# First two products of the cross-attention queries taken by pairs of feature blocks, with other durations in the planner

## The chip, the cores and the metric

The kernel runs on one core of a Trainium2 chip. The metric is the device time of one execution in microseconds (us); for each kernel several executions are timed and the median is given. The engines are named as in the profile: PE is TensorE (PEld its weight loads), DVE is VectorE, ACT is ScalarE, POOL is GpSimd, and SP is SyncE, which issues the DMAs here. A row of the trace such as `L193 MATMUL` names the line of the kernel that issued the instruction.

## The reference

One layer of a streaming-encoder trunk, with batch 1, 1024 rows, width 1024, in float32: token mixing by two groups of attention heads, cross-attention into 256 memory tokens, and an MLP of width 4096. Each of the three is normalised before, normalised after and added to the residual. The change lies in the second part, and in what stands beside it:

```python
def memory_cross_attention(h, mem_n, w_mq, w_mk, w_mv, w_mo):
    q = (h @ w_mq).reshape(B, S, MEM_HEADS, MEM_HEAD_DIM)       # 1024 x 1024 by 1024 x 1024, 4 heads of 256
    k = (mem_n @ w_mk).reshape(B, M, MEM_HEADS, MEM_HEAD_DIM)   # M = 256 memory tokens
    v = (mem_n @ w_mv).reshape(B, M, MEM_HEADS, MEM_HEAD_DIM)
    logits = einsum('bshd,bmhd->bhsm', q, k) * MEM_HEAD_DIM ** -0.5
    p = softmax(logits, axis=-1)
    o = einsum('bhsm,bmhd->bshd', p, v).reshape(B, S, D_MODEL)
    return o @ w_mo

x = x + rmsnorm(y @ w_out, g_mix_post)                          # end of the token mixing
h = rmsnorm(x, g_mem_pre)
y = memory_cross_attention(h, mem_n, w_mq, w_mk, w_mv, w_mo)
x = x + rmsnorm(y, g_mem_post)
```

## The kernel before

**Numbers in two parts.** Every operand of a product is split into a high part and a low part of a reduced format (fp32r). ScalarE copies the high part out, VectorE subtracts it for the low part, and `mm3` (lines 191 to 195) does three matmuls for each piece of a product: high by high, high by low, low by high. Names with `hi`, `_h` or `qh` are high parts, those with `lo`, `_l` or `ql` low ones.

**Rows.** The 1024 rows are 8 tiles of 128, in two halves of four (`th` is 0 and 1). When the output projection of the token mixing is done for a tile, `close_row` finishes it: GpSimd takes the inverse root `rw{n}0` of its mean square, VectorE adds to the residual (`xtw{n}`), the result is stored, ScalarE sums its squares, GpSimd takes a second root `rw{n}1`, and ScalarE scales the row to `yw{n}` (for the second half `yw10` to `yw13`, for the tiles 4 to 7). A root is two kinds of instruction, on lines 1088 to 1091, on 128 numbers. `raw_steps` transposes these rows on PE (`tr_h2T`: four transposes to a PSUM tile), and ScalarE copies them out as the raw query operands `h2r`. A residual row is loaded by the pump `Rows` into one of two buffers `xt`.

**Query projection.** The product `h @ w_mq` is taken as a Strassen-type scheme over a 2 x 2 division of both sides: seven half-size products instead of eight, in the order

```python
QUERIES = (("A11", "B11"), ("A12", "B21"), ("A22", "T4"), ("S2", "T2"), ("S1", "T1"), ("S4", "B22"), ("S3", "T3"))
for p, (an, bn) in enumerate(QUERIES):
    for i in range(2):          # a weight block: two feature blocks
        for a in range(2):      # feature block nb = 2 * i + a, 512 query columns
            for kc in range(4): # yields, then one mm3
```

The A and S names are forms of the queries (A11, A12 of the first 512 rows, A22 of the second, S1 to S4 sums of them, made and split by the pump `Forms`), the B and T names forms of the weights. So `mq00` to `mq03` are the four feature blocks of A11 by B11, each of 12 wide matmuls (128 x 512); blocks 0 and 1 read the weight block `B11_0`, blocks 2 and 3 `B11_1`. `query_leave` empties the PSUM tile: for product 0 ScalarE copies it to `qm`, for product 1 VectorE adds the two (`qv`), and `query_final` makes `qh` and `ql` of that, the queries of the first half of rows for head 0 (blocks 0 and 1) and head 1 (blocks 2 and 3).

**Attention to the memory.** For each half, head h and row tile b, `memory_score_steps` does six matmuls (`ms{th}{h}{b}`, 128 x 256) into one of two PSUM banks; VectorE takes the maximum, ScalarE the exponential with its sum (`mp`; its end frees the bank), VectorE the reciprocal, and GpSimd multiplies `mp` by it. `memory_turn_steps` transposes the pairs of tiles on PE (`mtr{th}{h}{0,1}`) and splits them into `ph2` and `pl2`. `memory_out_steps` multiplies them by the values (`mo{h}{nb}`), `operand_parts` copies the result out (`ro`, `A11o`, S forms), and `strassen_steps` does the output projection by seven products again (`ym`).

**What sets the order.** The order of instructions on each engine is written out by a planner in Python (`Flow`, lines 56 to 119), which simulates the program while it emits it. PE's work is a list of streams in order of priority; the planner takes the first stream whose next step is ready by its own clock. Work for other engines is put with a duration and a level, and a waiting item goes to its engine when that is free, the lowest level first. Pumps issue loads and splits when buffers are free: `stock.pump` loads the weight blocks in the order of `Stock.blocks` (`wraw`), ScalarE and VectorE split them (`whi`, `wlo`), and the homes of the split tiles (`w`, `w`, `wq`) are dealt in turn by place in that list. `Tokens` counts free buffers. So a duration in the text of the program decides order alone; on the chip each engine takes its instructions as written, and waits by semaphore where an operand is late.

From the end of the output projection on the streams are, in order of priority: `memory_out_steps`, `memory_turn_steps`, `memory_score_steps`, `rstd_steps`, the second half's rows and its filler (with `query_steps`, `strassen_steps` among it).

## Time and profile before

| | before |
|---|---|
| median of 3 runs | 1456.9 us (1456.2 to 1458.52) |
| the profiled execution | 1457.35 us |
| its span | 1455.6 us |
| granted clock of PE | 0.999 |
| instructions | 21887 |
| matmuls and transposes recorded on PE | 7505 |
| DMA | 262.12 MB, mean 180 GB/s |

The span is the profiled execution from its first instruction to its last; the execution's own time stands 1.75 us above it. The page gives each engine's busy time as a share of the span. Sections of 40 equal slices show it over time; one slice is 36 us here, so the change, which lies between 600 and 790 us, covers five of them. Two views carry more than the page for so small a stretch: the busy time of each engine between given times (columns: stretch; its length; then for PE, PEld, DVE, ACT, POOL the busy time and the number of instructions; the granted clock; the share of the DMA engines; GB/s), and the instructions of one engine in order of time (start, duration of one, engine, line, output <- inputs, shape, how many in a row, and in brackets the idle time of the engine ahead of it with what ended it).

### The profile page before, as it was taken

What the parts mean: (1) busy time and instruction counts of PE and PEld (TensorE: products, weight loads), DVE (VectorE), ACT (ScalarE), POOL (GpSimd) and SP (SyncE); (2) the same over time, 40 slices, a digit from 0 to 9 for tenths busy, and PEclk for the clock granted to TensorE, in tenths of its full rate; (3) what the DMA queues carried; (4) which work ended last, traced back from release to release, by engine and by line L of the source; (5) the groups of instructions that cost most, each with busy time, mean ns of one, the idle gap of its engine ahead of it and who ended that gap; (6) DMA issues with size and microseconds to landing.
All of it is one profiled execution on the core that took longest, in us unless ns stands there. A gap on an engine that the chain in (4) does not pass through costs nothing. (4 is left out here: it accounts for less than half of the span.)

```text
span 1455.6 us, 21887 instructions
## 1 busy us (share of the span) xinstructions
PE 1436.3 (99%) x7505; PEld 1222.9 (84%) x7505; DVE 1123.1 (77%) x1894; ACT 871.2 (60%) x1509; POOL 390.4 (27%) x496
## 2 busy tenths in 40 slices
PE   9999999999999999989999999999999999999998
PEld 8988888888889888877878887888888888888886
DVE  6788787867677857778888787896666866789897
ACT  6567676766677835975566555555555555555553
POOL 1245465545554311430103511003223000000003
PEclk9999999999999999999999999999999999999999
DMA  7143433542425584452134646875545997786786
GB/s 276 49 128 83 127 81 127 158 124 55 115 59 152 172 307 171 178 184 73 59 102 159 220 143 227 284 241 188 174 166 193 307 343 249 250 280 234 276 287 205
DMA packets 109439, 262.12 MB, mean 180 GB/s; under 512 B 12280, under 2 KB 30720, under 8 KB 109328
## 3 DMA queue, kind: packets, MB, share of 16 engines
q1 hardware_dynamic: 109184, 260.47, 53.8%
q8 instruction: 59, 0.97, 0.3%
q14 instruction: 52, 0.43, 0.1%
q10 hardware_dynamic: 144, 0.26, 0.1%
HBM read 186.70 MB, written 65.59 MB: 173 GB/s over the span
## 5 line engine op out<-in xcount | busy, mean ns | idle before, releaser
L727 DVE TENSOR_TENSOR phl<-ptr,phl 128x512 fp32r<-128x512 f32 (+1 forms) x152 | 92.3, 615 | 30.9 <-ACT phl L730 29.7
L730 ACT ACTIVATE phl<-ptr 128x512 fp32r<-128x512 f32 (+1 forms) x152 | 79.6, 539 | 49.4 <-PE ptr L721 47.7
L2454 ACT ACTIVATE whif<-ra 128x1024 fp32r<-128x1024 f32 x45 | 47.6, 1058 | 77.3 <-PE fx L194 34.8
L2589 POOL TENSOR_SCALAR rf<-sf 128x1 f32<-128x1 f32 x7 | 7.0, 1002 | 313.3 <-ACT jf L2570 313.1
L764 PE MATMUL pv<-phl,vs 128*128 128x512 f32 (+1 forms) x304 | 86.0, 367 | 0.4 <-DVE phl L727 0.4
L2456 DVE TENSOR_TENSOR wlof<-ra,whif 128x1024 fp32r<-128x1024 f32 x45 | 55.0, 1222 | 35.9 <-ACT whif L2454 35.8
L193 PE MATMUL fx<-vhif,whif 128*128 128x512 f32 x168 | 65.6, 391 | 0.0
L194 PE MATMUL fx<-vlof,whif 128*128 128x512 f32 x168 | 65.6, 391 | 0.0
L195 PE MATMUL fx<-vhif,wlof 128*128 128x512 f32 x168 | 65.4, 389 | 0.0
L764 PEld LDWEIGHTS pv<-phl,vs 128*128 128x128 f32 x304 | 54.8, 188 | 10.5 <-DVE phl L727 1.4
L778 POOL TENSOR_TENSOR o<-o 64x256 f32<-64x256 f32 x64 | 47.9, 749 | 51.6 <-DVE o L776 34.9
L2305 POOL TENSOR_TENSOR sc<-wf,wf 128x512 f32<-128x512 f32 x8 | 12.8, 1599 | 177.0 <-DMA gi1S<-s 90.9
L1528 POOL TENSOR_SCALAR mp<-mp,mst 128x256 f32<-128x256 f32 x32 | 20.0, 634 | 128.3 <-DVE mst L1527 82.3
L193 PE MATMUL k<-hT_hi,whik 128*128 128x512 f32 x128 | 53.3, 416 | 0.0
L193 PE MATMUL q<-hT_hi,whiq 128*128 128x512 f32 x128 | 51.8, 405 | 0.0
L776 DVE TENSOR_TENSOR o<-pv,o 64x512 f32<-64x512 f32 x64 | 43.9, 686 | 9.9 <-ACT o L781 8.9
L193 PE MATMUL yw<-whiwo,yT_hi 128*128 128x512 f32 x128 | 50.6, 396 | 0.0
L194 PE MATMUL k<-hT_lo,whik 128*128 128x512 f32 x128 | 50.3, 393 | 0.0
L195 PE MATMUL k<-hT_hi,wlok 128*128 128x512 f32 x128 | 50.3, 393 | 0.0
L194 PE MATMUL yw<-wlowo,yT_hi 128*128 128x512 f32 x128 | 50.3, 393 | 0.0
L194 PE MATMUL q<-hT_lo,whiq 128*128 128x512 f32 x128 | 50.2, 392 | 0.0
L195 PE MATMUL q<-hT_hi,wloq 128*128 128x512 f32 x128 | 50.2, 392 | 0.0
(786 smaller groups left out, 5282.1 us busy)
## 6 DMA issues: line engine op xcount, KB each, us to landing
wg<-in_w_ff SPq DMA_DIRECT2D x48, 512.0 KB, 6.0
ra<-gd SPq DMA_DIRECT2D x40, 512.0 KB, 3.8
wf<-in_w_ff SPq DMA_DIRECT2D x38, 512.0 KB, 3.8
wi<-in_w_ff2q SPq DMA_DIRECT2D x28, 512.0 KB, 5.7
gd<-s SPq DMA_DIRECT2D x32, 256.0 KB, 2.7
gd<-g SPq DMA_DIRECT2D x25, 256.0 KB, 2.8
wrawq<-in_w_qk SPq DMA_DIRECT2D x8, 512.0 KB, 4.2
wrawk<-in_w_qk SPq DMA_DIRECT2D x8, 512.0 KB, 3.7
```

The costliest lines, as they stand in the source:

```text
L193: nc.tensor.matmul(ps, lh, rh, start=start, stop=False, skip_group_check=more)
L194: nc.tensor.matmul(ps, lh, rl, start=False, stop=False, skip_group_check=more)
L195: nc.tensor.matmul(ps, ll, rh, start=False, stop=stop, skip_group_check=more)
L727: flow.put("V", at, 0.7, lambda: nc.vector.tensor_sub(pl[:, live, :], tr[:, live, :], f(ph[:, live, :])), done)
L730: flow.put("S", flow.end, 0.6, lambda ph=ph, tr=tr, live=live: nc.scalar.activation(ph[:, live, :], tr[:, live, :], AF.Copy), split)
L764: nc.tensor.matmul(pv[:, :, qs_, :], v, hl[:, :, hs, :], start=c == 0 and turn == 0, stop=last)
L776: flow.put("V", at, 0.7, lambda: nc.vector.tensor_add(o2[own], pv[own, :, :, ::step], o2[own]), lambda end: (free["pv"].give(end), flow.pu ...
L778: free["pv"].give(end), flow.put("G", end, 0.8, lambda: nc.gpsimd.tensor_add(o2[own, 0], o2[own, 0], o2[own, 1]), store)))
L1528: mul = lambda st=st, pr=pr: nc.gpsimd.tensor_scalar(pr, pr, st[:, 2:3], 1.0, op0=ALU.mult, op1=ALU.mult)
L2305: eng.tensor_sub(sc[:, k1], r0[:, k0], r1[:, k0])
L2454: nc.scalar.activation(ah, ra, AF.Copy)
L2456: nc.vector.tensor_sub(al, ra, f(ah))
```

## The change

1. **Order of the first two products.** A list `TURNS` of pairs (product p, weight block i) takes the place of the two loops: (0,0), (1,0), (0,1), (1,1), and from product 2 on both blocks of a product in turn, as before. The same list orders the loads of the weight blocks in `Stock.blocks`, so B11_0, B21_0, B11_1, B21_1 in place of B11_0, B11_1, B21_0, B21_1. The body of the loop is one level further out; the four tokens of a query form are given back after its second block.
2. **Durations of the planner.** The exponential of the scores 0.6 in place of 0.5, GpSimd's multiplication 0.7 in place of 0.5, the first root of a row 1.9 in place of 1.5, and a split query form counts as there at the end of its split instead of 0.5 after it.
3. **A second home of residual rows.** `Rows` may load the rows 6 and 7 into a tile of the pool `u4` where no `xt` buffer is free and 40 tiles of `u4` are. That pool is made with 30 tiles.

```diff
@@ -387,6 +387,8 @@
 
     QUERIES = (("A11", "B11"), ("A12", "B21"), ("A22", "T4"), ("S2", "T2"), ("S1", "T1"), ("S4", "B22"), ("S3", "T3"))
 
+    TURNS = [(p, i) for i in range(2) for p in range(2)] + [(p, i) for p in range(2, 7) for i in range(2)]
+
     def query_block(b, i):
         if b in qd:
             return qd[b][i]
@@ -417,7 +419,7 @@
             self.blocks += [(("wo", g, nh, i), row_pair(t["w_out"], 2 * g + i, nh), pair)
                             for g in range(2) for nh in range(2) for i in range(2)]
             where = {"B11": (0, 0), "B21": (2, 0), "B22": (2, 1)}
-            self.blocks += [(("mq", b, i), query_block(b, i), [P, 2, 4, P]) for _, b in QUERIES for i in range(2)]
+            self.blocks += [(("mq", QUERIES[p][1], i), query_block(QUERIES[p][1], i), [P, 2, 4, P]) for p, i in TURNS]
             for th in range(2):
                 self.blocks += [(("mo", th, nh, kp), row_pair(t["w_mo"], kp, nh), pair)
                                 for nh in range(2) for kp in range(4)] if th else [
@@ -1182,6 +1184,8 @@
 
                 self.parts.append((nb, call, then))
 
+    row_home = {}
+
     class Rows:
 
 
@@ -1189,15 +1193,22 @@
             self.left = [("w", n) for n in range(TB)] + [("m", n) for n in range(4)]
 
         def pump(self):
-            while self.left and free["xt"].ready():
+            while self.left:
                 nm, n = self.left[0]
-                if nm == "m" and not there(("x1d", n)):
+                home = "xt"
+                if nm == "w" and n > 5 and not free["xt"].ready() and free["u4"].ready(40):
+                    home = "u4"
+                if not free[home].ready() or nm == "m" and not there(("x1d", n)):
                     break
                 self.left.pop(0)
-                free["xt"].take()
-
-                def load(nm=nm, n=n):
-                    xin[nm, n] = p2.tile([P, D], F32, tag="xt", bufs=2, name=f"xt{nm}{n}")
+                free[home].take()
+                row_home[nm, n] = home
+
+                def load(nm=nm, n=n, home=home):
+                    if home == "u4":
+                        xin[nm, n] = u4(f"xt{nm}{n}", (P, D), F32)
+                    else:
+                        xin[nm, n] = p2.tile([P, D], F32, tag="xt", bufs=2, name=f"xt{nm}{n}")
                     nc.sync.dma_start(xin[nm, n], t["x"][n * P:(n + 1) * P, :] if nm == "w" else x1d[n])
 
                 flow.load(flow.now, load, mark(("xt", nm, n)))
@@ -1222,7 +1233,7 @@
                     ("S", 1.1, lambda: nc.scalar.activation(y, xin[nm, n], AF.Copy, scale=r[1])) if gnext == "mem" else
                     ("V", 1.3, lambda: nc.vector.scalar_tensor_tensor(y, xin[nm, n], r[1], gains[gnext],
                                                                       op0=ALU.mult, op1=ALU.mult))]
-            flow.chain(end, rest, lambda t_: (free["xt"].give(t_), then(t_)), 1)
+            flow.chain(end, rest, lambda t_: (free[row_home[nm, n]].give(t_), then(t_)), 1)
 
         def wait(end):
 
@@ -1231,7 +1242,7 @@
             else:
                 flow.put("G", end + 0.5, 0.0, lambda: None, wait)
 
-        flow.put("G", at, 1.5, lambda: root(0, ss[:, 0:1], ss[:, 1:2]), wait, 1)
+        flow.put("G", at, 1.9, lambda: root(0, ss[:, 0:1], ss[:, 1:2]), wait, 1)
 
     def mix_steps(g):
 
@@ -1408,7 +1419,7 @@
                 hi, lo = form_q[n][i], form_q[n][i + 2]
 
                 def then(end, i=i):
-                    seen["Q", n, i] = end + 0.5
+                    seen["Q", n, i] = end + 0.0
                     done(end)
                     if n in self.spent:
                         self.spent[n](end)
@@ -1449,36 +1460,37 @@
 
     def query_steps():
 
-        for p, (an, bn) in enumerate(QUERIES):
+        for p, i in TURNS:
+            an, bn = QUERIES[p]
             last = p in (1, 5)
-            for i in range(2):
...
-                    query_leave(p, nb, ps)
-                stock.done(("mq", bn, i))
-            for _ in range(4):
-                free["u4"].give(flow.end)
+            for a in range(2):
...
+                query_leave(p, nb, ps)
+            stock.done(("mq", bn, i))
+            if i:
+                for _ in range(4):
+                    free["u4"].give(flow.end)
 
     def query_leave(p, nb, ps):
         m, v, w, c = (acc.get((k, nb)) for k in "mvwc")
@@ -1527,10 +1539,10 @@
                     inv = lambda st=st: nc.vector.reciprocal(st[:, 2:3], st[:, 1:2])
                     mul = lambda st=st, pr=pr: nc.gpsimd.tensor_scalar(
                         pr, pr, st[:, 2:3], 1.0, op0=ALU.mult, op1=ALU.mult)
-                    flow.chain(flow.end, [("V", 0.43, top), ("S", 0.5, exp)],
+                    flow.chain(flow.end, [("V", 0.43, top), ("S", 0.6, exp)],
                                lambda at, inv=inv, mul=mul, key=("pm", th, h, b): (
                                    free["s"].give(at),
-                                   flow.chain(at, [("V", 0.17, inv), ("G", 0.5, mul)], mark(key), 0)), 0)
+                                   flow.chain(at, [("V", 0.17, inv), ("G", 0.7, mul)], mark(key), 0)), 0)
                 for _ in range(2):
                     free["q"].give(flow.end)
 
```

The number of instructions on each engine is the same in both kernels, and so is each instruction's kind and shape. Three places of the order follow. A row gives the line, the operation, output <- inputs with a running number to each name, and the shape; line numbers of the changed kernel are some 2 to 12 higher.

The first is VectorE's order from the residual addition of row 5 (`xtw5`) to that of row 7. `wlomq_B21_0` is the low part of a weight block, `qv0` the sum of the first two products for feature block 0, `ql000` and `ql001` the low parts of the queries of head 0. Before:

```order
L1216 SCALAR_TENSOR_TENSOR xtw5_7251<-yw11_6709,rw50_7383,xtw5_7251 128x1024
L465 TENSOR_TENSOR wlomq_B21_0_7400<-wrawmq_B21_0_6940,whimq_B21_0_7399 128x1024
L465 TENSOR_TENSOR wlomq_B21_1_7422<-wrawmq_B21_1_7281,whimq_B21_1_7421 128x1024
L1216 SCALAR_TENSOR_TENSOR xtw6_7412<-yw12_6710,rw60_7396,xtw6_7412 128x1024
L465 TENSOR_TENSOR wlomq_T4_0_7480<-wrawmq_T4_0_7404,whimq_T4_0_7479 128x1024
L1487 TENSOR_TENSOR qv0_7458<-mq10_7459,qm0_7344 128x512
L1216 SCALAR_TENSOR_TENSOR xtw7_7477<-yw13_6711,rw70_7418,xtw7_7477 128x1024
```

Now:

```order
L1227 SCALAR_TENSOR_TENSOR xtw5_7251<-yw11_6709,rw50_7385,xtw5_7251 128x1024
L467 TENSOR_TENSOR wlomq_B11_1_7397<-wrawmq_B11_1_6940,whimq_B11_1_7396 128x1024
L1499 TENSOR_TENSOR qv0_7406<-mq10_7407,qm0_7344 128x512
L467 TENSOR_TENSOR wlomq_B21_1_7419<-wrawmq_B21_1_7281,whimq_B21_1_7418 128x1024
L1458 SCALAR_TENSOR_TENSOR ql000_7441<-qv0_7406,qh000_7440 128x512
L1227 SCALAR_TENSOR_TENSOR xtw6_7412<-yw12_6710,rw60_7401,xtw6_7412 128x1024
L1499 TENSOR_TENSOR qv1_7434<-mq11_7435,qm1_7372 128x512
L467 TENSOR_TENSOR wlomq_T4_0_7472<-wrawmq_T4_0_7404,whimq_T4_0_7471 128x1024
L1458 SCALAR_TENSOR_TENSOR ql001_7487<-qv1_7434,qh001_7486 128x512
L1227 SCALAR_TENSOR_TENSOR xtw7_7483<-yw13_6711,rw70_7424,xtw7_7483 128x1024
```

`qv0` has moved ahead of the additions of rows 6 and 7, and `ql000`, `qv1` and `ql001` have come in between them.

The second is ScalarE's order around the scores of head 1 of the first half. `mp010` is the exponential of tile 0 of head 1, `ph200` the high part of the transposed first head, `A22q_h0` a half of the query form A22, `ro0` and `A11o0` the first head's result. Before:

```order
L1525 ACTIVATE mp002_7651,mst002_7650<-ms002_7643,mst002_7650 128x256
L1525 ACTIVATE mp003_7671,mst003_7670<-ms003_7663,mst003_7670 128x256
L1553 ACTIVATE ph200_7682<-mtr000_7684 128x2x256
L1416 ACTIVATE A22q_h0_7691<-h2r110_7470 128x1024
L1416 ACTIVATE A22q_h1_7692<-h2r111_7471 128x1024
L1525 ACTIVATE mp010_7707,mst010_7706<-ms010_7699,mst010_7706 128x256
L1553 ACTIVATE ph200_7682<-mtr001_7726 128x2x256
L1525 ACTIVATE mp011_7717,mst011_7716<-ms011_7709,mst011_7716 128x256
```

Now:

```order
L1457 ACTIVATE qh011_7691<-qv3_7627 128x512
L1627 ACTIVATE ro0_7694<-mo000_7699 128x512
L461 ACTIVATE whimq_T2_0_7719<-wrawmq_T2_0_7460 128x1024
L1427 ACTIVATE A22q_h0_7722<-h2r110_7476 128x1024
L1427 ACTIVATE A22q_h1_7723<-h2r111_7477 128x1024
L1629 ACTIVATE A11o0_7695<-ro0_7694 128x256
L1627 ACTIVATE ro0_7694<-mo001_7709 128x512
L1537 ACTIVATE mp010_7737,mst010_7736<-ms010_7729,mst010_7736 128x256
L1629 ACTIVATE A11o0_7695<-ro0_7694 128x256
L1537 ACTIVATE mp011_7747,mst011_7746<-ms011_7739,mst011_7746 128x256
```

The first head is finished (`ro0`, `A11o0`) ahead of the second head's exponentials, and a weight split and both A22 forms stand between its two results. On PE, in the same place, the order before was mq00, mq01, mq02, mq03, half of mq10, the transposes of rows 4 and 5, the rest of mq10, mq11, mq12, mq13, then ms000 to ms003 with the transposes of rows 6 and 7, mtr000, ms010, ms011, mtr001, ms012, ms013, mq20, mo000, mo001, mtr010. It is now mq00, mq01, mq10, mq11, half of mq02, the transposes of rows 4 and 5, the rest of mq02, half of mq03, ms000, ms001, the rest of mq03, half of mq12, ms002, ms003, mtr000, the rest of mq12, nine matmuls of mq13, the transposes of rows 6 and 7 with mtr001, the rest of mq13, mo000, mo001, ms010, ms011, ms012, three of mq20, ms013, mq20, mq21, mtr010.

The third is ScalarE's order around the scores of head 1 of the second half. `ym00` and `ym01` are copies of the output projection, `S2o0` and `S2o1` its operands. Before:

```order
L1729 ACTIVATE ym00_8463<-ym00_8462 128x512
L1553 ACTIVATE ph210_8537<-mtr100_8539 128x2x256
L1553 ACTIVATE ph210_8537<-mtr101_8546 128x2x256
L1525 ACTIVATE mp110_8561,mst110_8560<-ms110_8553,mst110_8560 128x256
L1729 ACTIVATE ym01_8465<-ym01_8500 128x512
L1592 ACTIVATE S2o0_8582<-ro0_7773 128x512
L1592 ACTIVATE S2o1_8583<-ro1_7896 128x512
L1525 ACTIVATE mp111_8573,mst111_8572<-ms111_8565,mst111_8572 128x256
```

Now:

```order
L1565 ACTIVATE ph210_8522<-mtr100_8524 128x2x256
L461 ACTIVATE whimo_0_T3_1_8564<-wrawmo_0_T3_1_8243 128x1024
L1537 ACTIVATE mp110_8540,mst110_8539<-ms110_8532,mst110_8539 128x256
L1741 ACTIVATE ym00_8459<-ym00_8458 128x512
L1537 ACTIVATE mp111_8553,mst111_8552<-ms111_8545,mst111_8552 128x256
L1565 ACTIVATE ph210_8522<-mtr101_8570 128x2x256
L1741 ACTIVATE ym01_8461<-ym01_8505 128x512
L1604 ACTIVATE S2o0_8582<-ro0_7694 128x512
L1604 ACTIVATE S2o1_8583<-ro1_7903 128x512
```

`mp111` has moved ahead of `ym01` and of the two S2 operands, and a weight split stands ahead of `mp110`.

45 lines of the change are left out of this document (22 added, 23 removed).

## The prediction

> **What bounds the kernel now.** The page comes first, then busy time by stretch, then TensorE's instructions in order of time wherever a pause is named.
>
> ```profile
> span 1455.6 us, 21887 instructions
> PE 1436.3 (99%) x7505; PEld 1222.9 (84%) x7505; DVE 1123.1 (77%) x1894; ACT 871.2 (60%) x1509; POOL 390.4 (27%) x496
> ```
>
> TensorE (PE) is busy 99% of the span, and the change takes no matmul away. It can win only pauses of PE, and only where it moves rows: PE's order differs from its row 3139 (616 us) to row 3947 (786 us).
>
> ```profile
> 600.00:620.00 20.00, 20.00 (x97) 16.68 (x96) 16.70 (x19) 18.66 (x33) 9.99 (x8) 1.00 0.52 193
> 620.00:660.00 40.00, 34.67 (x193) 28.59 (x192) 30.62 (x49) 29.86 (x62) 12.71 (x17) 1.00 0.43 153
> 660.00:730.00 70.00, 70.00 (x349) 58.84 (x348) 55.95 (x97) 36.98 (x69) 5.94 (x12) 1.00 0.22 68
> 730.00:760.00 30.00, 28.39 (x142) 23.21 (x141) 24.17 (x43) 19.72 (x38) 2.76 (x4) 1.00 0.35 106
> ```
>
> The second number is PE's busy time: 5.33 us are missing in 620 to 660, 1.61 in 730 to 760, none elsewhere here, and the granted clock (1.00) explains nothing. The pauses, with the engine that ended each:
>
> ```profile
> 625.08 1.86 PE L1338 MATMUL tr_h2T<-ident,yw 128*128 128x128 f32 x15 [1.98 <-ACT yw L1222]
> 642.73 0.39 PE L193 MATMUL ms<-km_hi,qh 128*128 128x256 f32 x1 [0.73 <-ACT mp L1525]
> 646.02 0.38 PE L193 MATMUL ms<-km_hi,qh 128*128 128x256 f32 x1 [1.17 <-ACT mp L1525]
> 649.76 0.51 PE L194 MATMUL mq<-A22q_l,whimq_T 128*128 128x512 f32 x1 [0.20 <-DVE A22q_l L1418]
> 655.88 0.44 PE L1550 MATMUL mtr<-ident,mp 128*128 128x128 f32 x2 [1.23 <-POOL mp L1528]
> 737.52 0.39 PE L193 MATMUL ms<-km_hi,qh 128*128 128x256 f32 x1 [1.47 <-ACT mp L1525]
> ```
>
> A pause costs more than its bracket, since matmuls start closer together than they last:
>
> ```profile
> 610.55 0.39 PE L193 MATMUL mq<-A11q_h,whimq_B 128*128 128x512 f32 x1
> 621.44 0.39 PE L193 MATMUL mq<-A12q_h,whimq_B 128*128 128x512 f32 x1
> 636.43 0.28 PE L193 MATMUL ms<-km_hi,qh 128*128 128x256 f32 x1
> 637.85 1.47 PE L1338 MATMUL tr_h2T<-ident,yw 128*128 128x128 f32 x12
> ```
>
> The first two rows are 48 matmuls apart: 0.227 us each, though one lasts 0.39. The last two are 12 apart: 0.118 for 0.28. So 0.16 of overlap is lost at each pause: 2.14 (0.16 more), 0.89, 1.33, 1.39 and 1.63. The A22 forms cost 0.47 in two rows, of which 0.36 is one matmul starting late. Together **6.2 us** in the first stretch and **1.6** in the second: 7.8 is the most that the change can win.
>
> **The change, part by part.** Edits that move nothing go first. The rows' second home needs 40 free tiles of a pool of 30, so it is never taken. The root's 1.9 and the query operands' 0.0 are planner figures; by the order they move single rows at most. All edits keep every instruction, so added work costs nothing; what counts is where PE meets unready data.
>
> *The first wait.* PE still does 54 matmuls of products before the transposes of rows 4 and 5 of the second half (row 3169 in both orders), so they come up at 622.8 as before. They wait for yw11, scaled by ScalarE once GpSimd has its root:
>
> ```profile
> 613.17 2.93 POOL L1090 TENSOR_SCALAR rw<-ssw 128x1 f32<-128x1 f32 x1
> 616.85 2.44 POOL L1090 TENSOR_SCALAR rw<-ssw 128x1 f32<-128x1 f32 x1
> 619.37 1.38 POOL L1091 TENSOR_TENSOR rw<-rw,mhalf 128x1 f32<-128x1 f32 x1
> 620.85 1.39 POOL L1090 TENSOR_SCALAR rw<-ssw 128x1 f32<-128x1 f32 x1
> 622.33 0.56 POOL L1091 TENSOR_TENSOR rw<-rw,mhalf 128x1 f32<-128x1 f32 x1
> 622.98 0.22 POOL L1088 TENSOR_SCALAR rw<-s2w 128x1 f32<-128x1 f32 x1
> 623.28 0.57 POOL L1091 TENSOR_TENSOR rw<-rw,mhalf 128x1 f32<-128x1 f32 x1
> 623.88 1.15 ACT L1222 ACTIVATE yw<-xtw,rw 128x1024 f32<-128x1024 f32 x1 [4.08 <-POOL rw L1091]
> ```
>
> One kind of operation on 128 numbers takes 0.22 or 2.93 us. It is long where VectorE runs operations with two SBUF inputs:
>
> ```profile
> 616.78 1.29 DVE L1216 SCALAR_TENSOR_TENSOR xtw<-yw,rw,xtw 128x1024 f32<-128x1024 f32 x1 [0.85 <-POOL rw L1091]
> 617.98 2.35 DVE L465 TENSOR_TENSOR wlomq_B<-wrawmq_B,whimq_B 128x1024 fp32r<-128x1024 f32 x2
> 620.79 1.29 DVE L1216 SCALAR_TENSOR_TENSOR xtw<-yw,rw,xtw 128x1024 f32<-128x1024 f32 x1 [0.45 <-POOL rw L1091]
> ```
>
> GpSimd's 616.85 ends at 619.29 and its 619.37 at 620.75, just after such operations end (first weight split about 619.2, second 620.33). The new order puts qv0 (one input in PSUM) after the first split: row 6's root can end near 619.9 instead of 620.75. But ql000 (two SBUF inputs, 0.69) then stands before row 6's addition, and qv1 behind it: VectorE is busy until about 623.5, then waits for ScalarE. GpSimd still owes four operations (0.22 and 0.56 twice). Where all four wait for 623.5, the last ends at 625.3 and yw11 at 626.5, 1.5 later than before; where they slip in between, yw11 comes 0.2 earlier. I take 0.5 later, nearer the middle since they slipped in at one of the boundaries above: **2.6 instead of 2.1**.
>
> The Trainium skill, page "SBUF — State Buffer", section "Who interferes with whom", says that a VectorE instruction with two SBUF inputs holds the read port GpSimd needs for the whole instruction, and whoever comes second fully blocks. The 2.93 against 0.22 agrees; taken strictly, it gives the late end, a rival below.
>
> *The scores of the second head.* Let T be when the transposes go on. PE's work from T to the end of mo000 is 48 wide matmuls, 24 of scores, 39 transposes (0.11 each: 0.27 long, spaced like the 16 of 625.08), and 0.09 at each of some eight changes of kind: 11.0 + 2.8 + 4.3 + 0.7 = 18.9. mo001 and two groups of scores follow, so ms012 comes up at T + 21.7. Its bank is free when mp010's exponential has read ms010. In ScalarE's new order that stands behind ro0, a weight split, two A22 forms, A11o0 and the second ro0:
>
> ```profile
> 643.43 2.09 ACT L1416 ACTIVATE A22q_h<-h2r 128x1024 fp32r<-128x1024 f32 x2
> 645.32 0.56 ACT L1525 ACTIVATE mp<-ms,mst 128x256 f32<-128x256 f32 x1
> 651.93 0.60 ACT L1615 ACTIVATE ro<-mo 128x512 f32<-128x512 f32 x1 [0.18 <-PE mo L195]
> 652.56 0.42 ACT L1617 ACTIVATE A11o<-ro 128x256 fp32r<-128x256 f32 x1
> 660.16 1.05 ACT L459 ACTIVATE whimq_T<-wrawmq_T 128x1024 fp32r<-128x1024 f32 x1
> ```
>
> From T + 19.1 it is 0.60 + 1.05 + 2.09 + 0.42 + 0.60 + 0.56 = 5.3, less about 0.1 of overlap at five joints: T + 23.9 to 24.4, a wait of 2.2 to 2.7. I take **2.4**; it replaces 0.89 and 1.33, the same kind. Bounds: 1.3 (today's wait) and 3.2.
>
> *Covered pauses.* A22's forms cost nothing now, since mo000 and mo001 (2.8 us) stand before their product; without that, 0.47. The multiplications mp010 to mp013, late today, now have product matmuls between exponential and transpose:
>
> ```profile
> 650.93 4.89 POOL L1528 TENSOR_SCALAR mp<-mp,mst 128x256 f32<-128x256 f32 x3 [0.51 <-DVE mst L1527]
> L1528 POOL TENSOR_SCALAR mp<-mp,mst x32: 477/480/1692, 640.6 to 783.2; 128x256 f32<-128x256 f32 x32
> ```
>
> Free, one takes 0.48; beside two-input work 1.69, so 1.2 is the price of a meeting. The first head's scores now come before row 7's addition has ended (its x row is loaded into a buffer that yw11 frees), leaving about 1 us of cover at ms002 and mtr000. I take nothing; bounds zero and two meetings, 2.4.
>
> *The second stretch.* At 737.5 PE waits for mp111, which ScalarE did behind ym01 and two S2 forms:
>
> ```profile
> 735.38 0.60 ACT L1729 ACTIVATE ym<-ym 128x512 f32<-128x512 f32 x1 [0.93 <-PE ym L195]
> 735.88 1.14 ACT L1592 ACTIVATE S2o<-ro 128x512 fp32r<-128x512 f32 x2
> 736.91 0.47 ACT L1525 ACTIVATE mp<-ms,mst 128x256 f32<-128x256 f32 x1
> ```
>
> Now mp111 stands before ym01, directly after ym00, with 12 wide matmuls and four transposes between ms111 and ms113. It waits for ym00's end and takes 0.6 + 0.47 of their 3.2 us, so the wait goes: **1.6 won**. A low part (pl210) now behind a weight split may cost 0.1.
>
> *Sum.* 6.2 + 1.6 - 2.6 - 2.4 - 0.1 = 2.7 us. The span becomes 1452.9 and the profiled execution, 1457.35, becomes 1454.65; it stands 0.45 above the median 1456.9, so the median to expect is **1454.2**.
>
> **The rivals.** *The early end:* row 5's root slips in (yw11 0.2 earlier) and ms012 waits only 1.3: 7.8 - 1.9 - 1.3 - 0.1 = 4.5 won, 1452.4. For it: today's wait was 1.3. Against: six ScalarE operations stand there, not two.
>
> *The port rule taken strictly:* T is 1.5 late, so 1.7 are won: 1455.2. For it: 613.17 waited through four operations. Against: 616.85 slipped in.
>
> *Slower, the multiplications:* GpSimd's multiplications meet VectorE's splits and sums more often, because both now fall in the same stretch. Four of 32 took over 1.3 us before, and one pause came of it. Each uncovered meeting costs 1.2: from three the gain is gone, from five it is slower by 3.3, 1460.2. Against: before most transposes stands a product of 1.4 us or more.
>
> **How the numbers follow.** About 0.2% (2.9 us) is what a measurement of this kernel tells from no change, so faster means below 1454.0. The forecast has 0.46, its own range 1453.1 to 1455.3, 0.20 of it below that line and 0.26 above; the early end 0.25 (faster); the strict rule 0.13 (same); the multiplications 0.16 (slower). Faster 0.45, same 0.39, slower 0.16. All good bounds at once win 4.5, all bad ones (T 1.5, 3.2, 2.4) lose: 7.8 - 3.6 - 3.2 - 2.4 - 0.1 = -1.5, or 1458.4. The three runs before differ by 2.3, so 0.5 is added at each end for where a median falls: the range is 1451.7 to 1458.9.
>
> **What would show it.** In the new profile the transposes' wait on yw should read 1.7 to 3.4; exactly one score matmul in the first stretch should wait on mp, by about 2.2; no wait on A22q_l; none on mp near 735. PE's missing time should be 4.5 to 5 in the first stretch and about 0.1 where 1.61 was. A second wait of PE on GpSimd, or one on a mo weight, would make it wrong.

## The result and the profile after

The changed kernel is faster: the ratio of its time to the kernel before is 0.9971, 95% interval 0.9963 to 0.9979. On 1456.9 us that is 4.2 us, between 3.1 and 5.4. Its median over 15 runs is 1454.9 us (1451.92 to 1457.7); the kernel before, run beside it and counted with the three runs shown earlier, has 1459.18 over 15 runs (1456.2 to 1460.05). The prediction was 1454.2 with a gain of 2.7. The profiled execution took 1455.35 us. The first line of its page, in which the five engines' own counts are those of before:

```profile
span 1453.6 us, 21873 instructions
```

The span is only 2.0 shorter than before, although the ratio says 4.2. The busy time by stretch, in the same stretches as before (stretch; length; busy time and count of PE, PEld, DVE, ACT, POOL; granted clock; DMA share; GB/s):

```profile
600.00:620.00 20.00, 20.00 (x97) 16.62 (x97) 16.70 (x19) 18.48 (x32) 9.69 (x8) 1.00 0.55 185
620.00:660.00 40.00, 35.72 (x196) 30.72 (x195) 27.24 (x45) 29.52 (x61) 11.50 (x17) 0.96 0.42 144
660.00:730.00 70.00, 70.00 (x349) 58.60 (x348) 59.59 (x105) 37.05 (x70) 6.18 (x11) 1.00 0.21 68
730.00:760.00 30.00, 29.86 (x150) 24.49 (x148) 24.93 (x41) 20.70 (x39) 5.33 (x6) 1.00 0.41 128
```

In the first stretch PE misses 4.28 us where it missed 5.33, in the second 0.14 where it missed 1.61. New is the clock of 0.96 in the second row: there was 1.00. (This execution also has a stretch of half clock from 11.58 to 15.00 us, far ahead of the change; its mq00 starts 0.30 later than before.) PE's instructions in order of time show two pauses left in the first stretch, and what follows the first of them:

```profile
625.65 3.19 PE L1349 MATMUL tr_h2T<-ident,yw 128*128 128x128 f32 x15 [2.24 <-ACT yw L1233]
629.45 0.40 PE L195 MATMUL mq<-A11q_h,wlomq_B 128*128 128x512 f32 x1
650.57 0.38 PE L193 MATMUL ms<-km_hi,qh 128*128 128x256 f32 x1 [2.04 <-ACT mp L1537]
```

The pauses are the two that the prediction kept: on yw11 (2.24, and 0.16 of lost overlap) and on mp010 (2.04, likewise). The second row shown is the third wide matmul behind the transposes, the third row the first matmul of ms012. But the 15 transposes behind the first one last 3.19 us where they lasted 1.86. From their start to the third wide matmul behind them (629.45) it is 3.80 us. In the profile of before the same way, from 625.08, ends here:

```profile
627.24 0.40 PE L195 MATMUL mq<-A12q_h,wlomq_B 128*128 128x512 f32 x1
```

That is 2.16, so 1.64 us were lost to something else than a wait. The busy time of the changed kernel in steps of 2 us names it:

```profile
624.00:626.00 2.00, 0.35 (x3) 0.35 (x4) 0.00 (x0) 1.55 (x2) 0.41 (x1) 1.00 0.43 174
626.00:628.00 2.00, 2.00 (x12) 2.00 (x11) 1.23 (x1) 2.00 (x5) 0.24 (x2) 0.50 0.59 96
628.00:630.00 2.00, 2.00 (x9) 1.75 (x9) 0.69 (x1) 2.00 (x6) 0.55 (x1) 0.65 0.95 358
```

The granted clock is 0.50 after the pause and full again from 629.40. The profile of before, with a pause of 1.98 in the same place, had 1.00 throughout.

One more pause is gone that the prediction left out. At the end of the stretch the transposes of the next stage ran in one piece; the first row is before, the second after:

```profile
795.00 1.86 PE L1301 MATMUL tr_h3T<-ident,ym 128*128 128x128 f32 x15 [0.39 <-DVE ym L1223]
```

```profile
792.48 1.91 PE L1312 MATMUL tr_h3T<-ident,ym 128*128 128x128 f32 x16
```

### The profile page after: what moved, and what is told of

It is laid out like the page before. It is cut to its first block, busy times and chain, and to the rows that moved or that the text cites. A ratio compares the mean times of both kernels' runs of the same rounds, so it can differ in the third digit from the quotient of the medians.

```text
span 1453.6 us, 21873 instructions
## 1 busy us (share of the span) xinstructions
PE 1437.0 (99%) x7505; PEld 1224.7 (84%) x7505; DVE 1125.0 (77%) x1894; ACT 871.9 (60%) x1509; POOL 391.5 (27%) x496
```

## The experiments

Waits trade places within this stretch: where one pause goes, another often grows. So besides the ratio one length is compared for all kernels: the time in the profile from the first matmul of mq00 (610.55 before) to the first matmul behind the 16 tr_h3T transposes (796.61 before), 186.06 us. Where the granted clock was below 1.00 in it, the loss is the sum over the windows of 10 us of (1 - clock) x 10.

| kernel | length, us | lost to the clock | ratio of times to before (95%) |
|---|---|---|---|
| before | 186.06 | 0 | |
| before_again | 187.71 | 1.7 | 1.0002 (0.9993 to 1.0011) |
| changed | 183.29 | 1.6 | 0.9971 (0.9963 to 0.9979) |
| fill_before | 186.11 | 0 | 0.9996 (0.9987 to 1.0005) |
| fill_after | 183.13 | 1.7 | 0.9970 (0.9959 to 0.9981) |
| turns | 186.61 | 1.7 | 0.9994 (0.9986 to 1.0003) |
| exp | 184.05 | 0 | 0.9991 (0.9983 to 1.0000) |
| past | 185.41 | 0 | 1.0002 (0.9993 to 1.0011) |
| no_exp | 189.42 | 3.4 | 1.0017 (1.0008 to 1.0026) |
| no_turns | 182.09 | 0 | 0.9973 (0.9964 to 0.9983) |
| late | 182.60 | 0 | 0.9974 (0.9964 to 0.9984) |
| hold9f | 182.77 | 0 | 0.9976 (0.9967 to 0.9984) |
| fill_hold | 182.74 | 0 | 0.9968 (0.9956 to 0.9980) |
| add6 | 187.12 | 1.7 | 1.0007 (0.9997 to 1.0016) |

(The changed kernel's 1.6 is the 1.64 worked out above.)

### The clock after a pause

The kernel before, once more, unchanged:

> The kernel before once more, unchanged, for a second profile. Its 15 runs stand at two levels, three near 1456.6 and twelve near 1459.2, and the one profile (1457.35) shows full clock throughout the stretch. Theory (clock): the upper level is the executions in which PE's clock is halved for about 3 us after its pause at 623, as the changed kernel's profile shows after its 2.24 us pause (15 transposes in 2.84 us, against 1.62). Then a profile near 1459 shows a granted clock of about 0.5 between 625 and 628, and one near 1456.6 shows 1.00 there. Rival (elsewhere): a profile near 1459 shows 1.00 there, and its extra 2.5 us lie in other stretches.

Its profiled execution took 1458.21 us. PE's transposes, and the busy time in steps of 2 us:

```profile
625.23 2.97 PE L1338 MATMUL tr_h2T<-ident,yw 128*128 128x128 f32 x15 [1.99 <-ACT yw L1222]
```

```profile
626.00:628.00 2.00, 2.00 (x12) 2.00 (x11) 1.23 (x1) 2.00 (x6) 0.00 (x0) 0.50 0.98 158
```

The pause is the same as in the first profile (1.99 against 1.98), but this time the clock went to 0.50 and the length grew by 1.65. So the same kernel with the same pause sometimes pays 1.7 us more, as the clock theory had it. In the sets of runs made for the experiments the kernel before ran 94 times: 49 runs have a mean granted clock of 0.999 or more and take 1457.0 on average, 45 have less and take 1458.8. (The 11 runs of before_again itself show it less well: three at 0.999 take 1458.4, eight below take 1458.9.) Of the changed kernel's 15 runs four are at 0.999 or more (mean 1452.4), eleven below (1455.2). The mean clock also counts the end of an execution, where PE has no work left and the clock is halved in every profile here. The profiles of no_turns and hold9f have no other stretch of half clock, and 0.998 all the same. So a mean below 0.999 is no sure sign of a dip.

Then the pause was filled with work that changes nothing, in the kernel before (18) and in the changed one (20):

```diff
+                if th == 1 and a == 0 and k == 0:
+                    for e in range(18):
+                        nc.tensor.transpose(tr[:, e // 2 % 2, e % 2, :], ident, ident)
```

> The kernel before with 18 transposes of the identity put ahead of the transposes of rows 4 and 5, into the same bank, which the real ones overwrite: 18 x 0.109 = 1.96 us, in a wait of 2.14. They change no result and wait for nothing new. Theory (clock): PE no longer pauses, the clock stays, nearly all runs stand at the lower level, 1456.6 against a median near 1459.2 for the kernel before: ratio 0.998. Rival (elsewhere): both levels stay as frequent, ratio 1.000. If the dummies themselves delay the transposes, 0.1 to 0.3 us slower than that.

> The changed kernel with 20 such transposes of the identity in the same place (2.18 us in a wait of 2.4). Theory (clock): all runs at the changed kernel's lower level, 1452.5; in the profile the 15 transposes take 1.6 us, not 2.8, at a granted clock of 1.00. Rival (elsewhere): 1455 as often as before, with the transposes fast.

In fill_before, ten of 11 runs have a mean clock of 0.999 and none is below 0.998, and its profile shows 1.00 after the filled pause:

```profile
626.00:628.00 2.00, 2.00 (x18) 1.91 (x16) 0.91 (x1) 2.00 (x5) 0.00 (x0) 1.00 0.69 94
```

The time moved by less than expected: median 1457.29 beside 1457.85, a ratio that no change would also give. In that set at most 11 of the 26 runs of the kernel before had the dip, by their mean clock, so there was about 11/26 of 1.7, or 0.7 us, to win, not 2.6; and the ten runs at 0.999 still differ by 2.75 us (1456.25 to 1459.0). So the clock theory holds for the 1.7, and the two levels that I had read out of the first 15 runs are not as clean as I took them. In fill_after the first pause was filled too, the transposes behind it ran at full clock, and the ratio is the changed kernel's (0.9970). The dip came behind the other pause:

```profile
648.00:650.00 2.00, 1.01 (x7) 1.00 (x8) 2.00 (x4) 1.71 (x6) 0.00 (x0) 1.00 0.00 0
650.00:652.00 2.00, 2.00 (x9) 1.77 (x8) 2.00 (x3) 0.10 (x2) 0.00 (x0) 0.51 0.00 0
```

That is the pause on mp010, so it is not a matter of the transposes. It is 2.04 as in the changed kernel's own profile, where no dip followed it. What decides can be read from the clock in the traces. Every dip lasts 3.41 us, and the full clock between two of them lasts a whole number of such windows: 40.96 us, or 12, in no_exp; 610.99, or 179, in the changed kernel. Where a profile has no dip, the windows can be counted back from the half clock at its end. Busy time by these windows, for before_again and then for the first profile of the kernel before:

```profile
622.38:625.79 3.41, 1.42 (x10) 0.97 (x9) 0.00 (x0) 1.76 (x3) 1.36 (x4) 1.00 0.61 241
625.79:629.20 3.41, 3.41 (x15) 3.20 (x14) 1.23 (x1) 3.41 (x9) 0.00 (x0) 0.50 0.88 210
```

```profile
620.41:623.82 3.41, 2.70 (x13) 1.91 (x11) 1.29 (x1) 0.00 (x0) 3.06 (x5) 1.00 0.90 320
623.82:627.24 3.42, 2.16 (x17) 2.08 (x18) 0.74 (x1) 3.36 (x6) 0.03 (x1) 1.00 0.43 99
```

In before_again the whole pause of 1.99 falls into one window, and the next has the half clock. In the first profile the end of a window divides the same pause into 0.71 and 1.26, and the clock stays. Between 600 and 800 us this fits all fourteen profiles: PE was idle for 1.99 to 3.06 us in the window ahead of each of the seven dips, and for 1.87 at most (hold9f) in any other window.

### Which edit made the gain

First the two main parts, each alone on the kernel before. turns takes the new order of the products (`TURNS`, the `Stock.blocks` line, the loop of `query_steps`) and no duration; exp takes these two:

```diff
-                    flow.chain(flow.end, [("V", 0.43, top), ("S", 0.5, exp)],
+                    flow.chain(flow.end, [("V", 0.43, top), ("S", 0.6, exp)],
...
-                                   flow.chain(at, [("V", 0.17, inv), ("G", 0.5, mul)], mark(key), 0)), 0)
+                                   flow.chain(at, [("V", 0.17, inv), ("G", 0.7, mul)], mark(key), 0)), 0)
```

> The kernel before with the new order of the first two products alone; the planner's durations as they were. Theory (two parts): this edit makes the first stretch and nothing else. In the profile PE waits 2.4 for yw and about 2.2 for mp010, while the waits of 1.63 near 737 and 0.55 near 795 stay as in the kernel before. Gain 6.2 + 0.5 of small pauses - 4.6 = 2.1 us, ratio 0.9986. Rival (one part): the new order carries the whole change, ratio 0.9971, and the durations nothing.

> The kernel before with the durations of the exponential (0.6) and of GpSimd's multiplication (0.7) alone. Theory (two parts): the first stretch stays (waits 2.14, 0.89, 1.33, 0.47, 1.39), and in the second the wait on mp111 (1.63) and the wait of the h3T transposes near 795 (0.55) are gone: gain 2.2 us, ratio 0.9985. Rival (one part): under 0.5 us, ratio 0.9997 or above, with a wait elsewhere in the second stretch.

Neither expectation held in full. PE's longer pauses under turns:

```profile
627.63 2.62 PE L1340 MATMUL tr_h2T<-ident,yw 128*128 128x128 f32 x15 [2.25 <-ACT yw L1224]
651.25 0.50 PE L194 MATMUL mq<-A22q_l,whimq_T 128*128 128x512 f32 x1 [0.51 <-DVE A22q_l L1420]
658.60 0.44 PE L1553 MATMUL mtr<-ident,mp 128*128 128x128 f32 x2 [0.31 <-POOL mp L1531]
667.51 0.50 PE L194 MATMUL mq<-S2q_l,whimq_T 128*128 128x512 f32 x1 [1.52 <-DVE S2q_l L1420]
740.37 0.38 PE L193 MATMUL ms<-km_hi,qh 128*128 128x256 f32 x1 [1.47 <-ACT mp L1528]
```

There is no pause on mp010: that one belongs to the interleaving and the durations together. In its place stands a new one on S2q_l of 1.52, and what was to be a gain of 2.1 is about 1.1 in the length without the dip (186.06 against 186.61 less 1.7), and not distinguishable in the times. Under exp the pause on mp111 near 737 is gone, as expected, and the one on A22q_l too; the one before tr_h3T stays (0.35), against the expectation. The length is 2.0 shorter; the ratio, 0.9991, shows a smaller gain than the 0.9985 expected, though its interval reaches to 0.9983.

Then the changed kernel without each part. no_exp has 0.5 and 0.5 again; no_turns has the old order with all of the planner's figures.

> The changed kernel without the durations of exponential and multiplication (0.5 and 0.5 again); the new order of the products, the root's 1.9 and the query operands' 0.0 stay. The order alone left PE waiting 1.69 us for S2q_l, since mo010 and mo011 stood between the halves of mq30; with the operands' 0.0 they stand ahead of mq30 whole. Theory (joint): the durations also order the first stretch once the products are interleaved, so this kernel waits on A22q_l (0.7) and a multiplication (0.5) as the order alone does, but no longer on S2q_l, and keeps the 1.63 near 737 and the 0.55 near 795: 0.9 + 1.7 = 2.6 us faster than the kernel before, ratio 0.9982. Rival (the operands' figure is nothing, as the prediction has it): 0.9994 as for the order alone, with the wait on S2q_l still there.

> The changed kernel with the old order of the first two products: all the planner's figures, and nothing of the interleaving. Theory (joint): about what the two durations do alone, waits near 737 and 795 gone and the first stretch nearly as before, ratio 0.9988 to 0.9992; so the interleaving is worth the rest to 0.9971, some 2.7 us, of which it shows only 0.9 alone. Rival (the figures alone): 0.9975 or less, the interleaving worth nothing beside them.

no_exp met neither its theory nor its rival; in no_turns the rival held, and that is the main finding. no_exp is slower than the kernel before, 1.0017. Its last great pause:

```profile
669.29 0.52 PE L195 MATMUL mq<-S2q_h,wlomq_T 128*128 128x512 f32 x1 [3.26 <-DVE wlomq_T L467]
```

The pause on S2q_l did go, and the same product now waits 3.26 us for the low part of its weight, whose high part ScalarE does behind the forms of S1, and whose low part VectorE does behind theirs. One dip of the clock follows it, and one the pause on yw (2.24). And no_turns, without the interleaving, is as fast as the whole change, as far as these runs can tell: 0.9973 beside 0.9971. These are its pauses over 0.2 us up to 750, all of them:

```profile
624.87 1.85 PE L1347 MATMUL tr_h2T<-ident,yw 128*128 128x128 f32 x15 [1.98 <-ACT yw L1231]
642.52 0.39 PE L193 MATMUL ms<-km_hi,qh 128*128 128x256 f32 x1 [0.73 <-ACT mp L1534]
644.71 0.44 PE L1559 MATMUL mtr<-ident,mp 128*128 128x128 f32 x2 [0.29 <-POOL mp L1537]
645.81 0.39 PE L193 MATMUL ms<-km_hi,qh 128*128 128x256 f32 x1 [0.66 <-ACT mp L1534]
```

Gone are the pauses on A22q_l, on the multiplications near 656, on mp111 near 737 and before tr_h3T; the length falls by 4.0 to 182.09. Its pause on yw was divided by a window's end in this execution (624.04), so in others no_turns may pay the dip as the kernel before does. The interleaving on top of that trades the four pauses shown (3.66 by the brackets) for the two of the changed kernel (4.28): without the dip the changed kernel's length would be 181.65, 0.4 better, and with it 1.2 worse.

The exponential and the multiplication alone gave 2.0 of the 4.0, so another figure has a share. past is the kernel before with the query operands' figure alone:

```diff
-                    seen["Q", n, i] = end + 0.5
+                    seen["Q", n, i] = end + 0.0
```

> The kernel before with one figure alone: a split query form counts as there at the end of its split, not 0.5 us after it. On PE this moves six rows: mo000 and mo001 stand behind the whole of mq20 instead of inside it, and three matmuls of mq21 stand ahead of mtr010 and mtr011. Theory (this figure takes the wait on GpSimd's multiplications): that wait of 1.39 near 656 shrinks to 0 to 0.7, all other waits stay, so 0.7 to 1.4 us faster, ratio 0.9990 to 0.9995; with the 0.9991 of the two durations alone this makes most of the 0.9973 of all figures together. Rival (single rows are worth nothing, as the prediction has it): the wait of 1.39 is only cut in two or moved, ratio 0.9998 or above.

```profile
656.19 0.44 PE L1550 MATMUL mtr<-ident,mp 128*128 128x128 f32 x2 [0.58 <-POOL mp L1528]
```

The bracket is 0.58 where it was 1.23, and the length 0.65 shorter, just below the expected range; all other pauses stay. The times cannot tell it from nothing (1.0002), as the rival had it. This figure puts three matmuls of mq21 ahead of mtr010; in no_turns three more stand between mtr010 and mtr011, and the pause is gone whole. The remaining 1.3 of the 4.0, what was left of this pause (0.74) and the one before tr_h3T (0.55), went only in the run with all figures. Neither the root's figure alone nor the operands' figure together with the two durations was run, so which of them takes this rest stays open. The ratios of exp and past say no more: together they come to 0.9993, with intervals 0.0017 and 0.0018 wide, beside the 0.9973 of all figures.

### Waits that only move

late holds back the transposes of rows 4 and 5 in the changed kernel:

```diff
-                       and ((th, 0) in raw_q or free["u4"].ready(4)))
+                       and ((th, 0) in raw_q or free["u4"].ready(4))
+                       and (th == 0 or a or k or flow.past(seen["h2", 5] + 2.6)))
```

> The changed kernel with the transposes of rows 4 and 5 of the second half held back in the planner by 2.6 us, so that 12 matmuls of the products (2.7 us) stand ahead of them that stood behind. Theory (the wait of 2.4 is real work that could stand there, and the clock dip hangs on it): the wait of PE on yw reads under 0.3, the clock stays at 1.00, and the time is 1452.5 - 2.4 = about 1450.1 in nearly all runs. Rival (the wait only moves): ms000 or a later step waits 2 us in its place, since ScalarE's and GpSimd's work behind is as late; then 1452.5, with the clock staying or not.

The rival held: the ratio is 0.9974, though the median, 1454.34, is not its 1452.5. The wait on yw is gone, the clock is 1.00 all through the stretch, and PE waits elsewhere:

```profile
627.85 0.39 PE L193 MATMUL ms<-km_hi,qh 128*128 128x256 f32 x1 [0.84 <-ACT qh L1458]
643.69 0.50 PE L193 MATMUL mo<-ph,vm_hi 128*128 128x512 f32 x1 [1.54 <-ACT h2r L1355]
649.32 0.39 PE L193 MATMUL ms<-km_hi,qh 128*128 128x256 f32 x1 [1.15 <-ACT mp L1538]
```

hold9f takes ScalarE's queue ahead of mp010 apart, in the changed kernel: the split of weight block T2_0 is put 9 us later, and the exponentials of head 1 of the first half go before other work (level -1).

```diff
-                flow.put("S", flow.now, 1.06, lambda key=key: self.hi(key), halves, 2)
+                flow.put("S", flow.now + (9.0 if key == ("mq", "T2", 0) else 0.0), 1.06, lambda key=key: self.hi(key), halves, 2)
...
-                                   flow.chain(at, [("V", 0.17, inv), ("G", 0.7, mul)], mark(key), 0)), 0)
+                                   flow.chain(at, [("V", 0.17, inv), ("G", 0.7, mul)], mark(key), 0)),  -1 if (th, h) == (0, 1) else 0)
```

> The changed kernel with two things moved on ScalarE in the first stretch: the weight split whimq_T2_0 is held back in the planner by 9 us, and the exponentials of head 1 go first, so that mp010 stands behind ro0, two A22 forms and one A11o0 only. Theory (the queue of ScalarE sets that wait, term by term): without the split (1.05), the second ro0 (0.60) and a neighbour the wait of PE on mp010 falls from 2.2 to about 0.6, and the kernel is 1.5 faster than the changed one: ratio to the kernel before 0.9961. Rival (another gate): the scores wait as long for something else, or the product with A22 or the one with T2_0 waits instead; ratio 0.9971 as for the changed kernel.

```profile
647.24 0.39 PE L193 MATMUL ms<-km_hi,qh 128*128 128x256 f32 x1 [0.60 <-ACT mp L1537]
651.29 0.50 PE L194 MATMUL mq<-A22q_l,whimq_T 128*128 128x512 f32 x1 [0.72 <-DVE A22q_l L1429]
655.32 0.44 PE L1562 MATMUL mtr<-ident,mp 128*128 128x128 f32 x2 [0.97 <-POOL mp L1540]
```

The wait on mp010 fell to 0.60 as worked out, so its size follows what ScalarE does ahead of it. But the 1.44 won there came back as 0.72 and 0.97, the very pauses that the prediction had called covered: 0.9976, no gain. fill_hold puts the 20 transposes of the identity in as well:

> The same, with 20 transposes of the identity put into PE's wait on yw (2.18 of 2.4 us), as in the fill_after run. Theory (clock): with neither pause over 1 us left the granted clock reads 1.00 from 600 to 1440 in the profile and 0.998 or more over every timed run, and the runs stand at the lower level alone: about 1450.8, ratio 0.9953 to 0.9960. Rival: the dip of the clock comes without a pause too, and the spread of runs stays at 4 us.

All of its six runs have a mean clock of 0.999 and lie within 1.4 us (1452.42 to 1453.82), so the steadiness came as expected; the time did not: 0.9968 beside the changed kernel's 0.9971. No kernel here is shown to be faster than the changed one.

add6 is a test of the meeting of GpSimd and VectorE. Row 6's addition is held back in the changed kernel:

```diff
-                flow.put("V", max(end, seen["xt", nm, n]), 1.3, add, store, 1)
+                flow.put("V", max(end, seen["xt", nm, n]) + (2.0 if (nm, n) == ("w", 6) else 0.0), 1.3, add, store, 1)
```

> The changed kernel with row 6's residual addition on VectorE held back in the planner by 2 us, so that it stands behind qv1, a weight split and ql001. In the changed kernel's profile the root of row 6 on GpSimd (622.00) takes 1.45 us beside that addition (621.75 to 623.03), and row 5's root is next in GpSimd's queue. Theory (the meeting on the port sets T): that instruction takes 0.57 instead, yw11 comes 0.9 earlier, PE's wait on yw reads 1.3 to 1.6 instead of 2.24, and the clock dips seldom: up to 1 us better than the changed kernel, ratio 0.9963 to 0.9970, if nothing behind waits for the later row 6. Rival (GpSimd is late whatever VectorE does): the wait stays at 2.2.

GpSimd's instructions of the changed kernel first, then of add6:

```profile
622.00 1.45 POOL L1093 TENSOR_TENSOR rw<-rw,mhalf 128x1 f32<-128x1 f32 x1
623.54 0.22 POOL L1090 TENSOR_SCALAR rw<-s2w 128x1 f32<-128x1 f32 x1
```

```profile
621.57 0.56 POOL L1093 TENSOR_TENSOR rw<-rw,mhalf 128x1 f32<-128x1 f32 x1
622.22 0.22 POOL L1090 TENSOR_SCALAR rw<-s2w 128x1 f32<-128x1 f32 x1
```

```profile
624.33 1.86 PE L1349 MATMUL tr_h2T<-ident,yw 128*128 128x128 f32 x15 [1.36 <-ACT yw L1233]
```

The instruction is row 7's root, not row 6's as the expectation has it; row 5's second root is next. It takes 0.56 in place of 1.45, with 0.69 us of an operation that reads PSUM (qv1) beside it instead of the 1.28 of the addition, and PE's wait is 1.36 in place of 2.24: the mechanism and its size held. The kernel is slower than the changed one all the same (1.0007 beside 0.9971), and the trace shows where: the addition now stands behind a split that waits 3.07 us for ScalarE, rows 6 and 7 come later, and PE waits 0.63, 1.26 and 0.82 for A22's forms and 1.63 and 0.76 for S2's.

## Why the prediction was right, and where it was not

The time, 1454.2, lies 0.7 below the median measured, and the gain, 2.7, below the 4.2 of the ratio and outside its interval (3.1 to 5.4). That the time came so near is in part luck: the kernel before, run beside the changed one, stood 2.3 above the 1456.9 from which the prediction started, and the gain was 1.5 above the one forecast, and the two nearly cancel. By the ratio the gain is clear of the 0.2% that the prediction asked of a faster kernel; by its line of 1454.0 the median is not. The lower end of the range, 1451.7, is 1451.9 by its own sum. The prediction's row numbers of PE (3139, 3169, 3947) are not the profile's, where these matmuls are rows 3410, 3440 and 4249; the times beside them are right. Step by step:

**The bound** held as far as pauses go. The most that the change could win was put at 7.8; it left out the pause before tr_h3T (0.55 with its lost overlap), which it had taken to lie outside, since PE's order is the same there. The traces put its end down to VectorE's order: between the two scalings (L1223 before) that these transposes read stood four other operations, in exp three, and in the changed kernel two.

**The first wait**, 2.6, measured 2.4. The working held too: T came 0.27 later counted from mq00 (yw11's scaling began at 624.45 against 623.88, and mq00 0.30 later), where 0.5 was taken. Of the four instructions that GpSimd still owed, two were drawn out by VectorE's work (the one at 622.00 to 1.45), and two ran in 0.22 and 0.57 once VectorE's last operation with two SBUF inputs was over (623.03). The Trainium skill, page "SBUF — State Buffer", section "SBUF: two separate sides", has GpSimd blocked for the whole of such an instruction where that started first; add6's 0.56 against 1.45 agrees, but the late end that the strict rule gave did not come, since only two of the four met such an operation.

**The scores of the second head**, 2.4, measured 2.2, on mp010 and on nothing else, as forecast. ScalarE's queue from the first ro0 to the end of mp010 took 4.65 (645.78 to 650.43), where 4.8 to 5.3 was taken. hold9f, which took the split and the second ro0 out of it together, shortened the wait by 1.44.

**Covered pauses**: in the changed kernel neither A22q_l nor a multiplication held PE up. hold9f shows by how little: 1.4 us earlier at the scores brings both back.

**The second stretch**: the pause on mp111 went, 1.6 with its overlap. The 0.14 that PE still misses there is a pause at 754.20 that stood at 756.24 before. No wait on pl210 shows. What was paid is another 0.14: a score matmul at 727.63 came late behind an exponential that ScalarE did after a weight split. PE's missing time in the first stretch is 4.28, a little under the 4.5 to 5 that the prediction named as its sign.

**Where the sum was short.** Without the dip the length shrank by 4.4 (186.06 - 181.65), 1.7 more than the 2.7. What was kept is 2.4 + 2.2 + 0.1 in place of 5.1: 0.4. The pause before tr_h3T is 0.55. The rest, 0.75, is delays of 0.05 to 0.2 at some dozen matmuls that stand behind a pause or beside it; the sum counted pauses with a bracket and the one on A22q_l alone. Against this stands the clock, which the sum had nowhere: 1.6 in the profiled execution, where the length shrank by 2.8 only.

**What failed** is the sentence that the root's 1.9 and the query operands' 0.0 "are planner figures; by the order they move single rows at most", which stands among the "edits that move nothing" and gives them no share in the sum. The single rows are the right ones: alone the operands' figure takes 0.65 of the 1.39 at the multiplications, and with the other durations all of it. The prediction gave no sum by edits, but it reads the first stretch as the interleaving's, and there it was wrong. The interleaving alone is 0.9994, the planner's figures without it 0.9973, and the whole 0.9971. The pauses that the likeliest case named came true. That the interleaving is what wins there did not: without it the gain is the same.

**The rivals.** The early end (4.5) is the nearest in size, but neither of its two conditions was met: yw11 was later, not earlier, and ms012 waited 2.2, not 1.3. The multiplications did take long more often (six of 32 took 1.30 or more, where it was four; the longest 1.88), in places that were covered.

## What to carry to other kernels

Where a planner writes the order, measure each of its figures alone and the change without it: two edits that look like one idea and some tidying can be the other way round, and a figure that moves six rows can hold the pause that matters. A pause on the critical engine that is taken away is often another one's cover, so the test is the length of the whole stretch, not the pause. And a profile is one execution: compare its clock with the other's before reading a difference of spans. Of the 4.2 us won, the spans show 2.0, and the dip of 1.6 accounts for most of the difference.

## What the runs showed of the hardware

PE's granted clock fell to half for 3.41 us at a time, at a cost of 1.7, after pauses of 1.99 to 3.26 us, and in add6 after two of 1.63 and 0.76 close together. It did not always fall: of the two profiles of the kernel before, both with this pause at 1.98 or 1.99, one shows it; and after one of 2.25 it stayed up in hold9f. The clock's records show a fixed grid of windows of 3.41 us whose place differs from one execution to the next. A dip came where PE was idle for 1.99 us or more of one window, and not where it was idle for 1.87 or less: the 2.25 of hold9f is divided at 625.01 into 1.87 and 0.38. One dip does not fit these figures: the one at 11.58 in the changed kernel's profile, with 1.57 us of idle time by the profile in its window, so 1.99 is no threshold for all work. The Trainium skill, page "TensorE: Matmul & The Clock Gate", section "Part 1: The HAM clock gate", states that the array goes to half clock after an idle window of about 3.4 us, that the windows run freely, and that it takes as long again to come back. The half clock, the grid and its 3.41 us agree; that the window has to be idle throughout does not: 1.99 us of it did here. Dummy transposes of 0.11 us kept the clock at 1.00 where they stood: with them ten of 11 runs of fill_before are at 0.999, and without them 49 of 94.
